# Attention scores: the keys' lower part laid twice over each other, so that both matmuls of a score use the same 128-row weights

## The chip, the core and the metric

One core of a Trainium2 chip runs the whole kernel. Its engines work through their own instruction lists side by side: TensorE (matmuls; its weight loads are listed apart), VectorE, ScalarE, GpSimd, and SyncE, which issues most of the DMA transfers. Times are device microseconds (us) of one execution; lower is better.

## The reference

One transformer block over 512 positions of width 1024, all in float32: a norm, a wide input projection, two branches (differential attention and a gated delta rule), a merge with gates, an output projection, an MLP and a gated embedding. The change is in the attention branch. It has 8 heads, each with two score maps of head size 64:

```python
s = jnp.einsum('bqhd,bkhd->bhqk', q_blk, k).astype(jnp.float32)
s = jnp.where(kpos[None, :] <= qpos[:, None], s, -jnp.inf)
w = jax.nn.softmax(s, axis=-1).reshape(b, DA_HEADS, 2, Q_BLOCK, t)
a = w[:, :, 0] - lam * w[:, :, 1]
return jnp.einsum('bhqk,bkhd->bqhd', a.astype(v.dtype), v)
```

The queries are worked through in 4 blocks of 128, and the scores are causal: block b needs the keys 0 to (b + 1) * 128.

## The kernel before, in words

Activations lie with channels on the 128 partitions and the 512 positions along the free dimension. Products that need float32 precision are made from float32r matmuls on split operands: a value is written as an upper part (`hi`) and a rest (`lo`). A dense tile (`dense_steps`) runs 8 times `hi` weights with `hi` and `lo` activations and then 8 times `lo` weights with `hi` activations, 24 matmuls of 512 columns. Weights come as `raw` by DMA from SyncE's queue (L106). In the long middle stage ScalarE casts the upper part (`whi`, L115) and writes its negative into `wlo` (L116), and a DMA from GpSimd's queue adds `raw` to it (L117).

The middle stage (up to about 790 us) mixes three kinds of work on TensorE in an order that the program writes out by its own estimate of matmul times (`run`, `step`, `fill`): the tiles of the input projection as filler, the attention of each head (`attn`), and the pieces of the delta rule (`gdn_a`, `gdn_i`, `gdn_u`, `gdn_s`, `gdn_n`). That order is fixed for TensorE; the other engines' lists and the addresses of the tiles are set by a scheduler and by memory pools.

A head h has 64 channels for score map s = 0 (partitions 0 to 63, `top`) and 64 for s = 1 (64 to 127, `bot`). `aq_tile` writes for each s a full tile `q[s]`: on the 64 partitions of s stands the upper part of q, on the other 64 its lower part. `ak_tile` writes for each s a full tile `kh[s]` (`k` in the rows): the upper part of k on its own 64 partitions (ScalarE, L679), and a copy of it on the other 64 (GpSimd, L681). So one 128-row matmul of `q[s]` with `kh[s]` gives q_hi k_hi + q_lo k_hi. The lower part of k stands in one tile `kl` (VectorE, L680), each s on its own 64 partitions, and a second matmul of only these 64 rows adds q_hi k_lo.

`attn` goes over b = 0 to 3 and, in it, over s: the two matmuls into a bank `psat` (at least 256 columns; the weights are 128 queries), a mask (L712), the row maximum (L713), and the exponential on ScalarE (L715). Then the two maps are combined into `aw`, transposed (`psaT`), copied to `aT` and multiplied with the values (`psao`). Between these steps the filler and the delta rule run. Right before b = 0 of a head, its `ak` tile has just been projected; the first score matmul waits for L679 to L681.

After the last head the remaining delta rule, 16 gate tiles (`gth`, stored in `g_d`) and the first loads of the next stage come together: `of`, the last head's output, is stored in `oa_d`; `ot` tiles are loaded from `oa_d` and split into `brh` (ScalarE, L98) and `brl` (VectorE, L99); the delta rule's `gdn_u` needs `Ye` and `Yx` (L533, L535) for its matmuls `psU`.

Of the kernel before, what the change touches and what calls it, by code (L numbers as in the profile page):

```python
# [8 lines left out]
F32 = mybir.dt.float32  # L9
F32R = mybir.dt.float32r  # L10
# [7 lines left out]
T = 512  # L18
# [19 lines left out]
def hybrid_block(ctx, tc, xT, pT, w1, wba, wa, wb, wo, wup, wdn, wple, wpg, vecs, rows, consts, out):  # L38
    nc = tc.nc
    V, S, PE, G = nc.vector, nc.scalar, nc.tensor, nc.gpsimd  # L40
    mult, add, sub, mx = ALU.mult, ALU.add, ALU.subtract, ALU.max
# [28 lines left out]
    def bc(ap, shape, axis):  # L70
        return ap.unsqueeze(axis).broadcast_to(shape)
# [3 lines left out]
    def mm(ps, lhsT, rhs, start=True, stop=True, **k):  # L75
        n = 1
        for i in rhs.shape[1:]:
            n *= i
        spent[0] += max(n / 2200.0, 0.025) if rhs.dtype == F32R else n / (1170.0 if k else 585.0)
        PE.matmul(ps, lhsT=lhsT, rhs=rhs, start=start, stop=stop, **k)  # L80

    def transpose(ps, src):
        mm(ps, src, ident, is_transpose=True)

    def rsqrt(pool, r, x, n):

        h = pool.tile([128, n], F32, name="nw_h")
        t = pool.tile([128, n], F32, name="nw_t")
        V.tensor_scalar(r.bitcast(I32), x.bitcast(I32), -0.5, 1597463007.0, op0=mult, op1=add)
        V.tensor_scalar(h, x, -0.5, None, op0=mult)  # L90
        for _ in range(3):
            V.tensor_tensor(t, r, r, op=mult)
            V.tensor_tensor(t, t, h, op=mult)  # L93
            V.scalar_tensor_tensor(r, in0=t, scalar=1.5, in1=r, op0=add, op1=mult)
# [61 lines left out]
    def newdense(src, a, kt=KD, lo=None, raw=None):  # L156
        w = load_w(src, kt, lo, raw)
        ps = pd.tile([128, T], F32, name="ps")
        dense(ps, w, a, kt)
        return ps  # L160
# [9 lines left out]
    with pool_("pro", bufs=2) as pool:  # L170
# [9 lines left out]
        for k in range(KD):  # L180
            q = ss if k == 0 else pool.tile([128, T], F32, name="sq")
# [12 lines left out]
        for d in range(KD):  # L194
            ps = newdense(wple[d], p2, 2, G, raw=raws[d] if d < 2 else None)
# [108 lines left out]
    apool = apool_.__enter__()  # L304
# [357 lines left out]
    at_ = {h: {} for h in range(8)}  # L662
# [11 lines left out]
    def ak_tile(h):  # L674
        def then(ps):
            kh = at_[h]["kh"] = [apool.tile([128, T], F32R, name=f"k{s}") for s in range(2)]
            kl = at_[h]["kl"] = apool.tile([128, T], F32R, name="kl")
            for s, hi, lo in ((0, top, bot), (1, bot, top)):
                S.copy(kh[s][hi], ps[hi])  # L679
                V.tensor_tensor(kl[hi], ps[hi], kh[s][hi].bitcast(F32), op=sub)  # L680
                G.tensor_copy(kh[s][lo], kh[s][hi])  # L681
        return ("ak", h), w1[8 + h], then, ("k_read", h - 1)

    def av_tile(h):
# [5 lines left out]
    def attn(h):  # L690
        d = at_.pop(h)
        q, kh, kl, vT = (d[n] for n in ("q", "kh", "kl", "vT"))
        psv = pt.tile([128, NC, 128], F32, name="psav", tag="t")
        for c in range(NC):
            transpose(psv[:, c], vT[:, c * 128:(c + 1) * 128])
        done.add(("av_read", h))
        vt = apool.tile([128, NC, 128], F32, name="vt", tag="vt")
        S.copy(vt, psv)
        oo = apool.tile([128, NC, 128], F32, name="oo")
        sso = apool.tile([128, NC], F32, name="asso")  # L700
        l2 = apool.tile([128, NC], F32, name="l2")
        yield 1.5
        for b in range(NC):
            n = (b + 1) * 128
            st = apool.tile([128, 4], F32, name="st", bufs=3)
            ws = []
            for s in range(2):
                pss = pt.tile([128, T], F32, name="psat", tag="t")
                m, hi, bs = max(n, 256), slice(64 * s, 64 * s + 64), slice(b * 128, n)
                mm(pss[:, :m], q[s][:, bs], kh[s][:, :m], stop=False)  # L710
                mm(pss[:, :m], q[s][hi, bs], kl[hi, :m], start=False)
                V.tensor_tensor(pss[:, b * 128:n], pss[:, b * 128:n], mqk, op=add)  # L712
                V.tensor_reduce(st[:, s:s + 1], pss[:, :n], axis=AX.X, op=mx, negate=True)  # L713
                w = apool.tile([128, T], F32, name="aw", bufs=3)
                S.activation(w[:, :n], pss[:, :n], AF.Exp, bias=st[:, s:s + 1], accum_out=st[:, 2 + s:3 + s])  # L715
                ws.append(w)
            if b == NC - 1:
                done.add(("k_read", h))

            rr = apool.tile([128, 1], F32, name="rr", bufs=3)  # L720
            V.reciprocal(rr, st[:, 3:4])
            V.scalar_tensor_tensor(rr, in0=rr, scalar=st[:, 2:3], in1=nlam, op0=mult, op1=mult)
            V.tensor_scalar(l2[:, b:b + 1], st[:, 2:3], st[:, 2:3], EPS, op0=mult, op1=mult)
            V.scalar_tensor_tensor(ws[0][:, :n], in0=ws[1][:, :n], scalar=rr, in1=ws[0][:, :n], op0=mult, op1=add)
            yield 6.0 + 0.5 * b
            psa = pt.tile([128, NC, 128], F32, name="psaT", tag="t")
            for kb in range(b + 1):
                transpose(psa[:, kb], ws[0][:, kb * 128:(kb + 1) * 128])
            aT = apool.tile([128, NC, 128], F32, name="aT", bufs=2)
            S.copy(aT[:, :b + 1], psa[:, :b + 1])  # L730
            yield 1.5
            pso = pt.tile([128, 128], F32, name="psao", tag="t")
            for kb in range(b + 1):
                mm(pso, aT[:, kb], vt[:, kb], start=kb == 0, stop=kb == b)
            V.tensor_copy(oo[:, b], pso)
            junk = apool.tile([128, 128], F32, name="ajunk")
            S.activation(junk, oo[:, b], AF.Square, accum_out=sso[:, b:b + 1])
            if b < NC - 1:
                yield 1.5
        V.scalar_tensor_tensor(sso, in0=sso, scalar=1.0 / 128.0, in1=l2, op0=mult, op1=add)  # L740
        rt = apool.tile([128, NC], F32, name="art")
        rsqrt(apool, rt, sso, NC)
        V.tensor_tensor(oo, oo, bc(rt, [128, NC, 128], 2), op=mult)
        yield 7.0
        psoT = pt.tile([128, T], F32, name="psaoT", tag="t")
        for c in range(NC):
            transpose(psoT[:, c * 128:(c + 1) * 128], oo[:, c])
        of = apool.tile([128, T], F32, name="of", tag="vt")
        S.activation(of, psoT, AF.Identity, scale=gsub)
        nc.sync.dma_start(oa_d[h], of)  # L750
# [8 lines left out]
    def units():  # L759
        for h in range(-1, 8):  # L760
            if h < 7:
                yield key_tile(h + 1)
                yield query_tile(h + 1)
                for i in range(2):
                    yield value_tile(h + 1, i)
                yield aq_tile(h + 1)
                yield av_tile(h + 1)
                yield ak_tile(h + 1)
            if h >= 0:
                yield gate_tile(h, 0)  # L770
                yield gate_tile(h, 1)
        for n in range(16):
            yield branch_gate(n)
# [3 lines left out]
    for h in range(8):  # L777
        chains.append([0.0, (("Z", h, 1), ("S", h)), gdn_n, h, ("B", h)])
        chains.append([0.0, (("U", h), ("B", h - 1)), gdn_s, h, ("S", h)])
        chains.append([0.0, (("I", h), ("U", h - 1)), gdn_u, h, ("U", h)])  # L780
        chains.append([0.0, (("ak", h), ("T", h - 1)), attn, h, ("T", h)])
        chains.append([0.0, (("V", h, 1), ("A", h - 1)), gdn_a, h, ("A", h)])
        chains.append([0.0, (("A", h), ("I", h - 1)), gdn_i, h, ("I", h)])
# [37 lines left out]
    h = hp.tile([128, KD, T], F32, name="h")  # L821

    with pool_("obp", bufs=1, side="right") as pool:
        b2 = branch(pool, ob_d, [*range(4, 8), *range(4)], pool, "ot", 2)
        m = []
# [4 lines left out]
        for d in range(KD):  # L830
            ps = pd.tile([128, T], F32, name="ps")
# [53 lines left out]
    for d in range(KD - NO):  # L885
        ps = newdense(wo[d], mg)
# [61 lines left out]
    for d in range(KD):  # L948
        ps = pd.tile([128, T], F32, name="ps")
# [16 lines left out]
    for d in range(KD - ND):  # L966
        ps = pd.tile([128, T], F32, name="ps")
# [38 lines left out]
    for sl in halves:  # L1006
        ss = new_ss()
        for d in range(KD):
            ps = pd.tile([128, T], F32, name="ps")
# [83 lines left out]
```

## Time and profile before

| | |
|---|---|
| time, median of 3 runs | 1423.91 us (1422.7 to 1426.05) |
| the profiled execution | 1418.5 us, of which its span 1416.7 us |
| mean granted TensorE clock | 0.985 of full speed |
| TensorE busy | 1343.1 us (95% of the span), 8402 matmuls |
| weight loads busy | 1101.9 us (78%) |
| VectorE busy | 801.6 us (57%) |
| ScalarE busy | 665.0 us (47%) |
| GpSimd busy | 213.6 us (15%) |

The profile lists what each engine did in one execution. Matmuls are pipelined: an entry's length reaches beyond the start of the next, so the distance from start to start is what a matmul takes of the stream. A weight load is an entry of its own (PEld) and can lie beside a running matmul. Idle time of an engine is put down to what ended it (the releaser).

### The profile page before, as it was taken

Reading aid. Unit: us, or ns where it says so; the run is one execution under the profiler, and the core shown is the slowest. Engines: PE = TensorE matmul, PEld = TensorE weight load, DVE = VectorE, ACT = ScalarE, POOL = GpSimd, SP = SyncE. Lnnn points to the kernel's source line nnn. Section 1 sums busy time; section 2 is a strip of 40 time slices with the busy share of each in tenths; the row PEclk is TensorE's granted clock in tenths of the full one; section 3 lists DMA queues with packets and bytes.
Section 4 is the critical chain, followed back from the end, with each engine's and each line's share of the span. In section 5 each row is a group of like instructions: output and inputs, shape, how many; then the busy total and the mean of one; then the engine's idle time right before and its main releaser. Section 6 shows DMA issues by size and latency. Waiting matters only on the chain.

```text
span 1416.7 us, 22558 instructions
## 1 busy us (share of the span) xinstructions
PE 1343.1 (95%) x8402; PEld 1101.9 (78%) x8402; DVE 801.6 (57%) x2132; ACT 665.0 (47%) x1354; POOL 213.6 (15%) x232
## 2 busy tenths in 40 slices
PE   6989999999999998999989999999999999999985
PEld 4767877777778776787768778898888888888985
DVE  6566695858768594876422443358443224434574
ACT  5656575666657574665545322254232223223241
POOL 3221111111211121120001000001421002200341
PEclk9999999999999999999989999999999999999997
DMA  7876555575655665574877753351122322323321
GB/s 258 186 185 140 140 138 145 142 172 135 163 137 132 146 138 144 130 162 118 228 181 186 247 184 120 118 194 53 52 98 90 102 92 90 98 96 104 111 83 60
DMA packets 94430, 194.65 MB, mean 137 GB/s; under 512 B 34000, under 2 KB 40528, under 8 KB 94320
## 3 DMA queue, kind: packets, MB, share of 16 engines
q1 hardware_dynamic: 81648, 147.07, 33.0%
q0 software_dynamic: 12672, 46.14, 17.6%
q8 instruction: 66, 1.08, 0.3%
q14 instruction: 44, 0.36, 0.1%
HBM read 130.19 MB, written 16.84 MB: 104 GB/s over the span
## 4 chain that ended last, share of the span: by engine, by line
PE 50%; DVE 5%; DMA 4%; ACT 1%; issue 1%; POOL 0%; SPq 0%; ACTq 0%; POOLq 0%; DVEq 0%
PE ps L80 45%; DMA ot<-ob_d 1%; DMA g_d<-gth 1%; DMA wlo<-raw 1%; DVE h L873 1%; DVE ht L872 1%; PE psat L80 1%; PE psS L80 0%; PE psO L80 0%; PE psV L80 0%; DVE ss L859 0%; PE psr L153 0%; PE psao L80 0%; PE pss L145 0%; DVE nw_t L93 0%
## 5 line engine op out<-in xcount | busy, mean ns | idle before, releaser
L80 PE MATMUL ps<-u_hi,whi 128*128 128x512 f32 (+1 forms) x952 | 384.3, 405 | 0.3 <-DVE mr L932 0.3
L80 PE MATMUL ps<-u_lo,whi 128*128 128x512 f32 (+1 forms) x952 | 371.5, 391 | 0.0
L80 PE MATMUL ps<-u_hi,wlo 128*128 128x512 f32 (+1 forms) x952 | 250.1, 396 | 4.3 <-DMA wlo<-raw 4.3
L80 PEld LDWEIGHTS ps<-u_hi,whi 128*128 128x128 f32 x952 | 180.9, 190 | 38.3 <-issue 2.1
L80 PEld LDWEIGHTS ps<-u_lo,whi 128*128 128x128 f32 x952 | 180.9, 190 | 33.3
L80 PEld LDWEIGHTS ps<-u_hi,wlo 128*128 128x128 f32 x952 | 173.0, 190 | 40.2 <-DMA wlo<-raw 5.5
L98 ACT CAST whi<-raw 128x1024 fp32r<-128x1024 f32 (+1 forms) x93 | 92.2, 993 | 228.3 <-PE ps L80 223.1
L99 DVE TENSOR_TENSOR wlo<-raw,whi 128x1024 fp32r<-128x1024 f32 x83 | 101.3, 1220 | 108.8 <-PE ps L80 88.2
L117 POOL DMA_DIRECT2D wlo<-raw x88 | 76.1, 864 | 491.5 <-ACT wlo L116 294.9
L115 ACT CAST whi<-raw 128x1024 fp32r<-128x1024 f32 x88 | 92.1, 1047 | 57.4 <-PE ps L80 56.0
L116 ACT ACTIVATE wlo<-whi 128x1024 fp32r<-128x1024 f32 x88 | 92.8, 1055 | 0.2
L80 PE MATMUL ps<-hid_hi,whi 128*128 128x512 f32 x224 | 88.5, 395 | 0.0
L80 PE MATMUL ps<-hid_lo,whi 128*128 128x512 f32 x224 | 88.4, 394 | 0.0
L80 PE MATMUL ps<-brh,whi 128*128 128x512 f32 x208 | 82.1, 396 | 0.5 <-ACT whi L98 0.5
L80 PE MATMUL ps<-brl,whi 128*128 128x512 f32 x208 | 82.1, 395 | 0.0
L369 DVE SCALAR_TENSOR_TENSOR acc<-ps,cw,acc 128x511 f32<-128x511 f32 (+2 forms) x96 | 71.3, 742 | 6.8 <-ACT acc L366 6.3
L934 POOL TENSOR_TENSOR mr<-mr 128x512 f32<-128x512 f32 (+1 forms) x37 | 39.3, 1063 | 216.6 <-ACT hid_hi L933 215.9
L932 DVE SCALAR_TENSOR_TENSOR mr<-ps,r 128x512 f32<-128x512 f32 (+1 forms) x37 | 22.9, 619 | 72.8 <-PE ps L80 69.3
L80 PE MATMUL ps<-hid_hi,wlo 128*128 128x512 f32 x224 | 56.9, 395 | 0.0
L80 PE MATMUL ps<-brh,wlo 128*128 128x512 f32 x208 | 52.6, 395 | 0.0
L80 PEld LDWEIGHTS ps<-hid_lo,whi 128*128 128x128 f32 x224 | 42.1, 188 | 10.3
L80 PEld LDWEIGHTS ps<-hid_hi,wlo 128*128 128x128 f32 x224 | 42.0, 188 | 10.3
(332 smaller groups left out, 2410.0 us busy)
## 6 DMA issues: line engine op xcount, KB each, us to landing
raw<-w SPq DMA_DIRECT2D x88, 512.0 KB, 3.5
wlo<-raw POOLq DMA_DIRECT2D x88, 512.0 KB, 4.8
raw<-wup SPq DMA_DIRECT2D x32, 512.0 KB, 3.3
raw<-wdn SPq DMA_DIRECT2D x32, 512.0 KB, 3.6
raw<-wb SPq DMA_DIRECT2D x16, 512.0 KB, 3.9
gB<-gcr_d SPq DMA_DIRECT2D x16, 256.0 KB, 4.2
bB<-ber_d SPq DMA_DIRECT2D x16, 256.0 KB, 4.9
ob_d<-zs SPq DMA_DIRECT2D x16, 256.0 KB, 3.6
```

The costliest lines, as they stand in the source:

```text
L80: PE.matmul(ps, lhsT=lhsT, rhs=rhs, start=start, stop=stop, **k)
L98: S.copy(hi, src)
L99: (eng or V).tensor_tensor(lo, src, hi.bitcast(F32), op=sub)
L115: S.copy(whi, raw)
L116: S.activation(wlo, whi.bitcast(F32), AF.Copy, scale=-1.0)
L117: nc.gpsimd.dma_start(wlo, raw, accum_op=add)
L369: V.scalar_tensor_tensor(acc[:, s:], in0=ps[:, :T - s], scalar=cw[:, j, w:w + 1], in1=acc[:, s:], op0=mult, op1=add)
L872: V.scalar_tensor_tensor(t, in0=psr, scalar=vec[:, g + d:g + d + 1], in1=y[:, d, sl], op0=mult, op1=mult)
L873: adds[d % len(adds)].tensor_tensor(h[:, d, sl], r, t, op=add)
L932: V.scalar_tensor_tensor(r[:, :n], in0=ps[:, :n], scalar=0.0, in1=r2[:, sl], op0=mx, op1=mult)
L934: G.tensor_tensor(r[:, :n], r[:, :n], r[:, :n], op=mult)
```

## The change

`kl` becomes two full tiles, `kl[0]` and `kl[1]`. Each holds the lower part of its score map's keys twice: on the 64 partitions where VectorE writes it, and, copied by GpSimd, on the other 64. The second matmul of a score then uses all 128 rows of `q[s]`, the same weights as the first. Beside q_hi k_lo it now adds q_lo k_lo, which the kernel before left out.

```diff
     def ak_tile(h):
         def then(ps):
             kh = at_[h]["kh"] = [apool.tile([128, T], F32R, name=f"k{s}") for s in range(2)]
-            kl = at_[h]["kl"] = apool.tile([128, T], F32R, name="kl")
+            kl = at_[h]["kl"] = [apool.tile([128, T], F32R, name=f"kl{s}") for s in range(2)]
             for s, hi, lo in ((0, top, bot), (1, bot, top)):
                 S.copy(kh[s][hi], ps[hi])
-                V.tensor_tensor(kl[hi], ps[hi], kh[s][hi].bitcast(F32), op=sub)
+                V.tensor_tensor(kl[s][hi], ps[hi], kh[s][hi].bitcast(F32), op=sub)
                 G.tensor_copy(kh[s][lo], kh[s][hi])
+                G.tensor_copy(kl[s][lo], kl[s][hi])
         return ("ak", h), w1[8 + h], then, ("k_read", h - 1)
...
-                m, hi, bs = max(n, 256), slice(64 * s, 64 * s + 64), slice(b * 128, n)
+                m, bs = max(n, 256), slice(b * 128, n)
                 mm(pss[:, :m], q[s][:, bs], kh[s][:, :m], stop=False)
-                mm(pss[:, :m], q[s][hi, bs], kl[hi, :m], start=False)
+                mm(pss[:, :m], q[s][:, bs], kl[s][:, :m], start=False)
```

TensorE's list has the same instructions in the same order before and after; only the height of 64 matmuls and their weight loads differs. The attention pool is larger by one tile of 128 x 512. The other lists change in a few places. On GpSimd, the first head's keys (`k`, `kl`), between two DMAs that finish weight tiles (`wlo`):

```order
 L117 DMA wlo_792<-raw_789 128x1024
 L681 COPY k_864<-k_864 64x512
-L117 DMA wlo_876<-raw_873 128x1024
+L682 COPY kl_866<-kl_866 64x512
+L117 DMA wlo_879<-raw_876 128x1024
 L681 COPY k_865<-k_865 64x512
+L682 COPY kl_867<-kl_867 64x512
 L429 TENSOR_TENSOR bB<-bB,dt 128x512
```

The weight DMA now stands behind the first `kl` copy, and the second `kl` copy behind the second `k` copy; the other seven heads read the same.

On ScalarE, behind the last head's output `of`, where the casts of `ot` (`brh`) meet the delta rule's `Yx` and `U`, first as it stood before:

```order
L749 ACTIVATE of<-psaoT,gsub 128x512
L98 CAST brh_8199<-ot 128x1024
L98 CAST brh_8201<-ot 128x1024
L115 CAST whi_8266<-raw_8264 128x1024
L755 ACTIVATE gth<-ps 128x512
L116 ACTIVATE wlo_8267<-whi_8266 128x1024
L115 CAST whi_8338<-raw_8336 128x1024
L98 CAST brh_8203<-ot 128x1024
L533 ACTIVATE Yx<-psY_8288,C 32x8x16
L98 CAST brh_8205<-ot 128x1024
L755 ACTIVATE gth<-ps 128x512
L533 ACTIVATE Yx<-psY_8288,C 32x8x16
```

and as it stands now:

```order
L750 ACTIVATE of<-psaoT,gsub 128x512
L115 CAST whi_8290<-raw_8288 128x1024
L756 ACTIVATE gth<-ps 128x512
L116 ACTIVATE wlo_8291<-whi_8290 128x1024
L98 CAST brh_8223<-ot 128x1024
L98 CAST brh_8225<-ot 128x1024
L115 CAST whi_8362<-raw_8360 128x1024
L533 ACTIVATE Yx<-psY_8312,C 32x8x16 x2
L756 ACTIVATE gth<-ps 128x512
L116 ACTIVATE wlo_8363<-whi_8362 128x1024
L542 COPY U_349<-psU_8370 16x8x16
L98 CAST brh_8227<-ot 128x1024
```

The first two casts moved from before a weight tile to behind it, and the third and fourth from before and between the two `Yx` to behind both. On SyncE's queue the first two loads of `ot` moved from ahead of the store of `of` to right behind it; on VectorE the third and fourth `brl` moved behind the `Ye` and the `U` copies.

## Rows read from the trace of the kernel before

**Rows 1.** Stretches: us, then busy (xcount) of each engine, TensorE's clock, DMA.

```profile
225.00:305.00 80.00, 77.19 (x599) 61.37 (x598) 57.72 (x193) 49.84 (x119) 12.61 (x15) 1.00 0.59 142
690.00:760.00 70.00, 63.48 (x501) 51.67 (x500) 19.44 (x48) 34.45 (x57) 7.74 (x9) 0.93 0.75 199
```

**Rows 2.** Waits of TensorE, 60 to 700 us: total us, times, longest.

```profile
PE psN L80 <- DVE vs L613: 3.9, 4, 1.7
...
PE ps L80 <- DMA wlo<-raw: 3.4, 2, 2.0
PE psat L80 <- POOL k L681: 3.4, 5, 1.6
...
PE psq L80 <- ACT kt L415: 0.3, 1, 0.3
```

**Rows 3.** Instructions on tile kl: ns min/median/max, first and last start, shapes.

```profile
L80 PEld LDWEIGHTS psat<-kl,q x64: 182/183/183, 86.9 to 674.8; 64*128 64x128 f32 x64
...
L680 DVE TENSOR_TENSOR kl<-ps,k x16: 682/689/695, 84.8 to 631.9; 64x512 fp32r<-64x512 f32 x16
```

**Rows 4.** Timeline of TensorE, two score blocks: start us, length us, instruction.

```profile
102.24 0.28 PE L80 MATMUL psat<-k,q 128*128 128x256 f32 x1
102.45 0.38 PE L80 MATMUL psat<-kl,q 64*128 64x256 f32 x1
102.77 0.38 PE L80 MATMUL psat<-k,q 128*128 128x256 f32 x1
...
103.39 0.50 PE L80 MATMUL ps<-u_hi,whi 128*128 128x512 f32 x1
103.73 0.40 PE L80 MATMUL ps<-u_lo,whi 128*128 128x512 f32 x1
103.96 0.39 PE L80 MATMUL ps<-u_hi,whi 128*128 128x512 f32 x1
...
346.22 0.40 PE L80 MATMUL psat<-k,q 128*128 128x512 f32 x1
...
347.83 0.50 PE L80 MATMUL ps<-u_hi,whi 128*128 128x512 f32 x1
```

**Rows 5.** Timeline of TensorE and its weight loads, 256 columns, delta rule.

```profile
669.56 0.28 PE L80 MATMUL psS<-Sh,kql 128*128 128x256 f32 x1
669.56 0.19 PEld L80 LDWEIGHTS psS<-Sl,kqh 128*128 128x128 f32 x1
669.67 0.28 PE L80 MATMUL psS<-Sl,kqh 128*128 128x256 f32 x1
...
669.79 0.28 PE L80 MATMUL psS<-Sh,kqh 128*128 128x256 f32 x1
```

**Rows 6.** Timeline of all engines where a head's first score block starts.

```profile
383.01 0.60 POOL L681 CAST k<-k 64x512 fp32r<-64x512 f32 x1 [5.42 <-ACT k L679]
...
383.18 0.68 DVE L680 TENSOR_TENSOR kl<-ps,k 64x512 fp32r<-64x512 f32 x1
...
384.26 0.85 POOL L117 DMA_DIRECT2D wlo<-raw  x1 [0.64 <-ACT U L542]
...
385.16 0.61 POOL L681 CAST k<-k 64x512 fp32r<-64x512 f32 x1
...
386.44 0.50 PE L80 MATMUL ps<-u_hi,whi 128*128 128x512 f32 x1
```

**Rows 7.** Timelines of SyncE, ScalarE, VectorE and TensorE behind the last head.

```profile
697.40 1.24 SPq L750 DMA_DIRECT2D oa_d<-of  x1
...
702.39 0.59 SPq L805 DMA_DIRECT2D ot<-oa_d  x1
...
709.28 1.04 ACT L98 CAST brh<-ot 128x1024 fp32r<-128x1024 f32 x1 [3.79 <-DMA ot<-oa_d]
710.35 1.23 DVE L99 TENSOR_TENSOR brl<-ot,brh 128x1024 fp32r<-128x1024 f32 x1 [5.46 <-ACT brh L98]
...
714.12 0.21 PE L80 MATMUL psU<-U,Yx 128*16 128x16 f32 x1 [1.86 <-ACT Yx L533]
```

## The prediction

> **What bounds the kernel now.** I read the busy time by stretch first [rows 1]. In a stretch that holds one attention head, 225 to 305 us, TensorE is busy 77.19 of 80 us, VectorE 57.72, ScalarE 49.84 and GpSimd 12.61: TensorE sets the pace, the others have room. The same view shows one weaker stretch, 690 to 760 us, just behind the last head: TensorE 63.48 of 70 us at a mean granted clock of 0.93.
>
> The waits of TensorE from 60 to 700 us come next [rows 2]. The largest item is 3.9 us; the list has 15, down to 0.3 us, and adds up to about 26 us. So in the attention stage a microsecond taken out of TensorE's own stream is mostly a microsecond of the span, if the stream really holds it. One item bears on the change: 3.4 us, five waits of the score matmuls for GpSimd's copies of `k`.
>
> Then the score matmuls themselves. The 64 matmuls with `kl` are 64 rows high, each with a weight load of its own of 183 ns [rows 3]; their neighbours are all 128 rows. The stream in order of time shows what this height does [rows 4]. A score block (both `s` of one `b`, four matmuls) of 256 columns starts at 102.24 and the next tile at 103.39: 1.15 us. Within it the starts are 0.21, 0.32 and then twice some 0.31 us apart (102.77 to 103.39). In a row of 128-row matmuls of the same 256 columns, each also with new weights, the starts are 0.11 to 0.12 us apart [rows 5]. There the load of the next weights (0.19 us) begins at the start of the matmul before and lies beside it; with `kl` the distance is the load plus the columns, 0.19 + 0.12 = 0.31: nothing lies beside. At 512 columns a block takes 346.22 to 347.83 = 1.61 us [rows 4], while dense matmuls of 512 columns start 0.23 us apart (103.73 to 103.96). So each change of height, into 64 rows and back out, costs one uncovered load, and it trails into the next tile: 103.39 to 103.73 is 0.34 instead of 0.23.
>
> **The change, part by part.**
>
> *Height.* All four matmuls become 128 rows high. A block of 256 columns then takes 4 x 0.12 = 0.48 instead of 1.15 us: 0.67 saved. At 512 columns 4 x 0.23 = 0.92 instead of 1.61: 0.69. I take 0.67 for each of the 32 blocks (8 heads, 4 `b`), and set the 8 blocks with b = 0 aside, because there GpSimd decides. 24 x 0.67 = 16.1 us. The trail behind a block, 0.34 - 0.23 = 0.11, goes where a 128-row float32r matmul follows; I count 15 such blocks, 15 x 0.1 = 1.5 us. That both matmuls now name the same weights is counted at nothing: dense pairs use the same weights twice already and still start 0.23 us apart. Bounds of this part: the full 32 x 0.67 + 32 x 0.11 = 25 us, and 0 if the load stays uncovered (a rival below).
>
> *Two more copies for each head.* The upper and lower half of `kl` are now each copied to the other half by GpSimd, 16 copies of the same kind as those of `k`, 0.6 us each. GpSimd's order becomes k, kl, weight DMA, k, kl. One head stands for the pattern [rows 6]. The first `k` copy begins at 383.01, VectorE's first `kl` ends at 383.86, so its copy runs to about 384.55; the weight DMA, at 384.26 before, begins about 384.6 and ends 385.45; the second `k` copy ends about 386.1, the second `kl` copy about 386.7. TensorE's last score matmul then starts at 386.8 and the next tile at 386.9, where it started at 386.44: this block loses 0.5 us. The same sum on the other seven heads gives +0.3, +0.25, +0.15, +0.15, 0, -0.1, and -0.5 for the head whose copies are long done. Together about +0.7 us. TensorE runs its list in order, so behind the waiting matmul stand the dense matmuls of the weight tile in work, and nothing else can step in. The weight DMA issued 0.35 us late is not counted: two waits for `wlo` in 620 us make 3.4 us in all [rows 2], so it normally lands early. VectorE's `kl` subtraction takes 682 to 695 ns in all 16 cases [rows 3], whether GpSimd copies beside it or not, so I price slower VectorE at 0, and at most at the copies' own length, 16 x 0.61 = 9.8 us.
>
> *What is late next.* A chain of VectorE and ScalarE work that spans a score block loses up to 0.67 us of cover, since its own length stays. Nothing if every chain had that much slack, all 16.9 us if none had. The list [rows 2] has about 20 waits of this kind against many more places where TensorE meets such a chain without waiting; I take one block in five, 3.4 us given back, near the end that the 96% busy TensorE speaks for.
>
> *The last head's tail.* The pool for attention is larger by one tile, and loads and splits of `ot` move there. Before, TensorE stood until 714.12 for `Yx` [rows 7]: ScalarE runs `Yx` behind a cast of `ot` that began at 709.28, on data whose load was issued at 702.39, 6.9 us earlier. After, the first two loads of `ot` are issued behind the store of `of` (issued at 697.40, 1.24 us), so at about 698.7, land 6.9 us later at 705.6, and their two casts of 1.04 us end at 707.7. VectorE's subtractions of 1.23 us each (row of 710.35) end at about 709.1, and the two `Ye` and `Yx` follow without another `ot` between them. TensorE goes on at about 710 instead of 714.1: about 4 us. The clock there (0.93 in the mean of 70 us, so part of the time at 1.2 instead of 2.4 GHz) may drop for as long as before. I take -3.5; the bounds are -7, if stall and clock loss both go, and +2, if the loads land later than I assume.
>
> *Order on VectorE elsewhere.* In the first head one `aw` moves behind an instruction that waits for a load; a `Uq` step or a transpose changes place with a neighbour in others. All feed waits that TensorE had there anyway, so they are priced at 0, with 2 us either way.
>
> **Sum.** -16.1 - 1.5 + 0.7 + 3.4 - 3.5 = -17.0 us. The profiled execution took 1418.5 us (span 1416.7, and 1.8 around it), so 1401.5 by its measure. The median of the runs is 5.4 us above it: 1423.91 - 17.0 = 1406.9, say 1407 us.
>
> **A rule that speaks against it.** Two 128-row matmuls with different weights follow each other at 0.12 us with the load inside that time [rows 5]. The Trainium skill says otherwise in one place: TensorE: Matmul & The Clock Gate, part 3 on packing small matmuls, has weight loads overlap matmuls in flight only when their row groups differ. By that rule a matmul on all 128 rows could never cover the next load, the distance would stay 0.31, and the first term would be 0 in place of 16.1. The rows disagree with it, so I go by the rows.
>
> **The rivals.**
>
> *Most of it is given back.* TensorE's time goes but chains become the bound: VectorE is at 57.72 of 80 us per head and has instructions waiting on each other. If three blocks in five hand their 0.67 back, 10.1 instead of 3.4 us, and the tail brings nothing, the change is -6.8: 1417 us. For it: the waits of TensorE are nearly all for VectorE, ScalarE and DMA. Against it: they total only 4% of the stage.
>
> *No cover, slower.* The uncovered load may come from the score tiles themselves (their weights `q`, their target banks) and not from the height. Then the first term is 0, and in seven of the eight b = 0 blocks the last matmul comes 0.61 us later because its `kl` copy stands behind the second `k` copy: +4.3 us with the tail as it was, 1428 us. It decides from the point where less than some 0.2 us of a block is saved. For it: the `k` matmul between two `kl` also starts 0.3 us after its neighbour. Against it: that is the first of 128 rows after one of 64, and the 128-row matmuls of `psS` run at 0.12 [rows 5].
>
> *Larger than thought.* All 32 trails and blocks count, no chain is late, and the tail frees its whole stall: -25 - 0 - 7 with the copies at +5 is about -27, 1397 us.
>
> **How the numbers follow.** My forecast, with its own range 1400 to 1413, gets 0.73; the give-back 0.15; the larger gain 0.07; no cover 0.05. The range for 8 in 10 is 1399 to 1416 us: it reaches into the give-back and leaves out the far ends. What a measurement of this kernel can tell from no change is about 0.2%, 2.8 us. Faster by more than that: forecast, larger gain and nearly all of the give-back, 0.93. Within: 0.03, from the rest of the give-back. Slower: 0.04, from no cover.
>
> **What would show it.** Right: no 64-row matmul on the score tiles; within a block from b = 1 on, starts 0.12 us (256 columns) and 0.23 us (512) apart; in b = 0 blocks the wait for GpSimd moved to the last matmul and longer by 0.3 to 0.6 us; a head some 2 us shorter; TensorE's wait for `Yx` in the tail ending earlier. Wrong: distances of 0.31 us between 128-row score matmuls; TensorE's waits for VectorE and ScalarE grown by more than 7 us over the stage; or a new wait of several microseconds in the tail.

## The result and the profile after

The changed kernel takes 1409.51 us (median of 4 runs, 1404.96 to 1412.98); the kernel before, on the same chip, 1423.47 us (1422.7 to 1426.05). The ratio is 0.9897, interval 0.9866 to 0.9928: 14.0 us faster. Two more comparisons of the same pair gave 0.989 (0.9854 to 0.9926; 15.8 us) and 0.9881 (0.9855 to 0.9908; 17.9 us). Predicted were 1407 us and -17.0, with a range of 1399 to 1416. The profiled execution of after took 1404.96 us (span 1403.2), 13.5 less than that of before.

The page's line of busy times, after (engine, busy us, share of the span, instructions):

```profile
PE 1326.9 (95%) x8402; PEld 1101.2 (78%) x8402; DVE 803.1 (57%) x2132; ACT 664.0 (47%) x1354; POOL 223.0 (16%) x248
```

There are as many matmuls as before; TensorE is busy with them for 16.2 us less, and GpSimd is busy for 9.4 us more, with the copies. The score tiles by name, after: line, engine, operation, count, then min/median/max ns, first and last start, shapes:

```profile
L80 PE MATMUL psat<-kl,q x64: 277/337/582, 84.1 to 664.5; 128*128 128x256 f32 x32, 128*128 128x384 f32 x16, 128*128 128x512 f32 x16
```

No score matmul is 64 rows high any more. A block of 256 columns in TensorE's list of after (start us, length, line, operation, shape, columns), where [rows 4] had 1.15 us:

```profile
165.97 0.28 PE L80 MATMUL psat<-k,q 128*128 128x256 f32 x1
166.09 0.28 PE L80 MATMUL psat<-kl,q 128*128 128x256 f32 x1
166.21 0.28 PE L80 MATMUL psat<-k,q 128*128 128x256 f32 x1
166.33 0.28 PE L80 MATMUL psat<-kl,q 128*128 128x256 f32 x1
166.45 0.28 PE L80 MATMUL psS<-Sh,kqh 128*128 128x256 f32 x1
```

And one of 512 columns, where it was 1.61 us:

```profile
343.57 0.40 PE L80 MATMUL psat<-k,q 128*128 128x512 f32 x1
343.81 0.40 PE L80 MATMUL psat<-kl,q 128*128 128x512 f32 x1
344.04 0.40 PE L80 MATMUL psat<-k,q 128*128 128x512 f32 x1
344.27 0.39 PE L80 MATMUL psat<-kl,q 128*128 128x512 f32 x1
344.51 0.39 PE L80 MATMUL ps<-u_hi,whi 128*128 128x512 f32 x1
344.74 0.40 PE L80 MATMUL ps<-u_lo,whi 128*128 128x512 f32 x1
```

The blocks take 0.48 us (165.97 to 166.45) and 0.94 us (343.57 to 344.51). The tile behind the second goes on at 0.23 us: there is no trail. Over all 32 blocks, from the first score matmul to the next other one and waits inside included, before takes 47.5 us and after 34.7. Of this the 8 blocks with b = 0 take 13.7 us before and 14.8 after, the other 24 take 33.7 and 19.9. The matmuls at their own pace (0.12, 0.175 and 0.232 us for 256, 384 and 512 columns) would be 20.7.

The head of [rows 6], after, on GpSimd, TensorE and the DMA it issues (in brackets the idle time before and what ended it):

```profile
379.59 0.60 POOL L681 CAST k<-k 64x512 fp32r<-64x512 f32 x1 [5.41 <-ACT k L679]
380.51 0.61 POOL L682 CAST kl<-kl 64x512 fp32r<-64x512 f32 x1 [0.32 <-DVE kl L680]
381.09 0.85 POOL L117 DMA_DIRECT2D wlo<-raw  x1
381.99 0.61 POOL L681 CAST k<-k 64x512 fp32r<-64x512 f32 x1
382.54 0.62 POOL L682 CAST kl<-kl 64x512 fp32r<-64x512 f32 x1
...
382.65 0.39 PE L80 MATMUL psat<-k,q 128*128 128x256 f32 x1 [0.87 <-POOL k L681]
383.22 0.39 PE L80 MATMUL psat<-kl,q 128*128 128x256 f32 x1 [0.17 <-POOL kl L682]
383.44 0.39 PE L80 MATMUL ps<-u_hi,whi 128*128 128x512 f32 x1
```

The order is the predicted one: k, kl, weight DMA, k, kl. The last score matmul waits for the last copy.

What TensorE waits for from 60 to 690 us, after (who waits, for whom: us in total, times, longest), against [rows 2]:

```profile
PE psN L80 <- DVE vs L613: 6.5, 4, 3.0
PE psat L80 <- POOL k L681: 4.9, 5, 1.8
PE psaoT L80 <- DVE eq L478: 4.1, 1, 4.1
...
PE psat L80 <- DVE oo L736: 1.9, 1, 1.9
...
PE psat L80 <- POOL kl L682: 1.1, 6, 0.2
```

The whole list grows from 26.1 to 33.4 us: the waits of `psat` from 4.1 to 8.8, the other waits for VectorE and ScalarE from 18.6 to 23.2.

The tail, after ([rows 7]), from the lists of SyncE's queue, ScalarE and TensorE:

```profile
684.98 0.32 SPq L751 DMA_DIRECT2D oa_d<-of  x1
685.46 1.10 SPq L806 DMA_DIRECT2D ot<-oa_d  x2
...
693.14 1.05 ACT L98 CAST brh<-ot 128x1024 fp32r<-128x1024 f32 x1 [1.91 <-DMA ot<-oa_d]
694.76 1.06 ACT L98 CAST brh<-ot 128x1024 fp32r<-128x1024 f32 x1 [0.57 <-DMA ot<-oa_d]
...
697.44 0.21 PE L80 MATMUL psU<-U,Ye 128*16 128x16 f32 x2 [1.06 <-DVE Ye L535]
698.61 0.19 PE L80 MATMUL psU<-U,Yx 128*16 128x16 f32 x1 [0.18 <-ACT Yx L533]
```

TensorE stands there for some 1.6 us in all, before for 6.5. From the end of the last score matmul to the last matmul into `psY`, also of the delta rule, it is 43.9 us, before 49.8. The clock of the 70 us there is 0.98, against 0.93 in [rows 1].

### The profile page after: what moved, and what is told of

Its sections match the earlier page's. It is cut to its first block, busy times and chain, and to the rows that moved or that the text cites. A ratio compares the mean times of both kernels' runs of the same rounds, so it can differ in the third digit from the quotient of the medians.

```text
span 1403.2 us, 22583 instructions
## 1 busy us (share of the span) xinstructions
PE 1326.9 (95%) x8402; PEld 1101.2 (78%) x8402; DVE 803.1 (57%) x2132; ACT 664.0 (47%) x1354; POOL 223.0 (16%) x248
## 4 chain that ended last, share of the span: by engine, by line
PE 44%; DVE 4%; DMA 4%; issue 1%; ACT 1%; SPq 0%; POOL 0%; ACTq 0%; POOLq 0%; DVEq 0%
PE ps L80 41%; DMA ot<-ob_d 1%; DMA g_d<-gth 1%; DVE h L874 1%; DMA wlo<-raw 1%; DVE ht L873 1%; DMA ot<-oa_d 1%; DVE ss L860 0%; PE psr L153 0%; DVE brl L99 0%; PE pss L145 0%; ACT brh L98 0%; DVE nw_t L93 0%; DVE nb_r L94 0%; PE psO L80 0%
```

## The experiments

The changed kernel differs from before in three things at once: the height of the second matmul, the copies of `kl`, and a pool with one more tile, which reorders the lists. The first batch (before at 1425.93 us) takes them one at a time.

### The pool alone: kl in two tiles, still 64 rows

```diff
-kl = apool.tile([128, T], F32R, name="kl")
+kl = [apool.tile([128, T], F32R, name=f"kl{s}") for s in range(2)]
...
-mm(pss[:, :m], q[s][hi, bs], kl[hi, :m], start=False)
+mm(pss[:, :m], q[s][hi, bs], kl[s][hi, :m], start=False)
```

> The kernel before with kl in two tiles of 128 x 512 instead of one, each used only on its own 64 partitions: matmuls 64 rows high as before, no copies of kl. Only the attention pool grows, and with it the lists of the other engines change as they do in the changed kernel, the tail behind the last head included. Theory (the height is the gain, the tail a small extra): score blocks still 1.15 us at 256 columns, TensorE's stall for Yx in the tail shorter, 2 to 6 us faster than before, about 0.997. Rival (the order of the lists made most of the gain): 10 us or more faster, 0.993 or below. Rival (the order brings nothing): 1.000.

Measured: 1419.3 us, ratio 0.9962 (0.9938 to 0.9985). The medians differ by -6.6 us; the ratio would make it -5.4. Its blocks take 49.6 us as a sum, much as before. The tail is short here too: from the last score matmul to `psY` 43.7 us. TensorE's list of this kernel, `psU`:

```profile
710.20 0.21 PE L80 MATMUL psU<-U,Ye 128*16 128x16 f32 x2 [0.68 <-DVE Ye L535]
```

So some 5 to 7 us of the gain have nothing to do with the weights. They come with the order of loads and casts that the larger pool brings; the tail alone is 6.1 us shorter in this profile.

### The height alone: zeros in the other half, no copies

Against the changed kernel:

```diff
+kls = [apool.tile([128, T], F32R, name=f"kl{s}") for s in range(2)]
+G.memset(kls[s][lo].bitcast(F32), 0.0)          # once
...
-G.tensor_copy(kl[s][lo], kl[s][hi])
```

> The changed kernel without its copies of kl: the two kl tiles are allocated once, the half that VectorE doesn't write is filled with zeros once at the start, and the 128-row matmul adds zero there (so q_lo k_lo is left out as it was before). Theory (height): blocks of 0.48 us at 256 columns as in the changed kernel, and in the first block of each head no wait for kl: 0.1 to 0.5 us less there for each of seven heads, 2 to 3 us faster than the changed kernel, about 0.988 of before. Rival (the copies cost much more, by holding up the weight DMAs behind them): 6 us or more faster than the changed kernel, 0.985 or below. Rival (the copies cost nothing, since the block waits for the copy of k anyway): the same as the changed kernel, 0.990.

Measured: 1405.78 us, 0.9865 (0.9842 to 0.9889), -20.2 us. Against `two64`, which has as large a pool and was run in the same batch, the height is worth 13.5 us. The blocks fall from 49.6 to 29.9 us. (The tiles with zeros are also allocated once and not for each head; no run takes this apart.)

### The copies alone: changed kernel with 64-row matmuls

```diff
-mm(pss[:, :m], q[s][:, bs], kl[s][:, :m], start=False)
+mm(pss[:, :m], q[s][hi, bs], kl[s][hi, :m], start=False)
```

> The changed kernel with its copies of kl, but the second matmul reads only the 64 rows of its own half, as before (nothing reads the copied halves). Theory (height): blocks of 1.15 us again; no matmul waits for the copies, so they cost only GpSimd's time: as fast as the kernel with two tiles and no copies within 2 us, about 0.997 of before. Rival (copies hold up weight DMAs): 3 us or more slower than that kernel, 1.000 or above.

Measured: 1419.02 us, 0.9961 (0.9939 to 0.9983): the same as `two64`. 16 copies on GpSimd cost nothing that these medians can tell, as long as no matmul waits for them.

### Same weights, or same height?

The 64-row pairs are grouped by height, k, k, kl, kl; the same grouping with 128 rows (and zeros) takes away neighbours with equal weights.

```diff
+for s in range(2): mm(psc[s][:, :m], q[s][:, bs], kh[s][:, :m], stop=False)
+for s, hi in ((0, top), (1, bot)): mm(psc[s][:, :m], q[s][hi, bs], kl[s][hi, :m], start=False)   # group64
+for s, hi in ((0, top), (1, bot)): mm(psc[s][:, :m], q[s][:, bs], kl[s][:, :m], start=False)     # group128
```

> 64-row matmuls in two tiles without copies, but in each block both 128-row matmuls first, then both 64-row matmuls (rows 0 to 63, then rows 64 to 127). Theory (what costs is the change of height): only two changes in a block instead of four; starts at 256 columns about 0.12, 0.21, 0.12 and 0.31 us apart, a block of 0.76 us, 0.35 us less than before in 24 or more blocks, 8 to 10 us faster than the kernel with two tiles. Rival (a 64-row load is never covered): the third distance is 0.31 as well, a block of 0.95. Rival (the load of another group of rows runs beside the matmul): third distance 0.12 or below. The first exponential of a block starts later by one matmul, which may give 1 or 2 us back.

> The kernel with zeros in the other half of kl (128 rows, no copies of kl), but in each block both matmuls with k first, then both with kl: no two neighbours have the same weights any more. Theory (height): still 0.12 us from start to start at 256 columns and 0.23 at 512, blocks of 0.48 and 0.93 us. Rival (the same weights are what saves): a load of 0.19 us uncovered between the matmuls, 0.31 us apart, blocks near 1.1 us and 12 us or more slower than the kernel with zeros. The first mask and exponential of a block start one matmul later, so a time 0 to 3 us above the kernel with zeros, about 0.988 of before.

Measured: `group64` 1410.05 us, 0.9897 (0.9872 to 0.9922). `group128`, in the second batch (before 1424.25 us), 1405.7 us, 0.9873 (0.9842 to 0.9903), against 1405.78 for `zero` in the first batch and 1402.56 for the same kernel in the third (`zero2`, below). A block of `group128` in TensorE's list (x2: two matmuls drawn together):

```profile
167.37 0.40 PE L80 MATMUL psat<-k,q 128*128 128x256 f32 x2
167.61 0.40 PE L80 MATMUL psat<-kl,q 128*128 128x256 f32 x2
167.85 0.28 PE L80 MATMUL psS<-Sh,kqh 128*128 128x256 f32 x1
```

Four matmuls in 0.48 us, as in after, though no neighbour uses the weights of the one before: that both matmuls of a score name the same weights is worth nothing in the block. A block of `group64`, matmuls and weight loads (PEld):

```profile
238.37 0.40 PE L80 MATMUL psat<-k,q 128*128 128x256 f32 x2
...
238.69 0.19 PEld L80 LDWEIGHTS psat<-kl,q 64*128 64x128 f32 x2
238.69 0.38 PE L80 MATMUL psat<-kl,q 64*128 64x256 f32 x2
239.00 0.19 PEld L80 LDWEIGHTS ps<-U,Y 128*64 128x64 f32 x2
```

0.64 us where I expected 0.76. The two 64-row matmuls take 0.32 us together, a load of 0.19 and one matmul's 0.12: they lie side by side, one on the upper and one on the lower rows. This is the second rival of the expectation, a load that runs beside the matmul of another group of rows. The Trainium skill, TensorEngine Tiling (Array Packing), Key Properties, says that a change of tiling mode drains TensorE, and that different tiles can load and multiply in parallel. The rows agree with both. In these rows a block that changes height four times costs 0.67 us more than one of full height, and one that does so twice 0.16 more (0.64 against 0.48), with the 0.12 us already taken off that the two matmuls side by side save.

### What the copies cost the changed kernel

The changed kernel was run in three comparisons and the version with zeros in two; the third (before 1424.16 us) has both at once.

> The changed kernel once more, on the same chip as the three beside it. All theories: 0.990 of before, within 0.003.

> The changed kernel beside the kernel with zeros on one chip, to tell what its copies of kl cost. All theories: 0.990 of before, within 0.003.

> The kernel with zeros beside the changed kernel. Theory (the copies cost the waits for kl in seven first blocks, 0.4 us each, and the order on VectorE in the first head): 2 to 4 us faster than the changed kernel. Rival (nothing, as something else holds TensorE in those blocks): within 1 us of it.

Measured: the changed kernel 1408.41 (`again`) and 1406.27 us (`again2`); `zero2` 1402.56 us, 0.9836 (0.9811 to 0.9862), 3.7 us below `again2`. It is the fastest version here. The two intervals still overlap a little; over all executions the changed kernel has a mean of 1408.0 us (16) and the version with zeros 1403.4 (11). TensorE's `psat` waits sum to 8.7 us in `again2` and 5.2 in `zero2`, about the difference. But 1.9 us of it is one wait for `oo` in the first head; `two64`, which has no copies, waits 1.4 us there, so this part may be the order of the lists and not the copies. `zero2` leaves out q_lo k_lo, as the kernel before does.

### Attempts to buy cover

With `zero`, the largest wait is `psN` for `vs` (6.8 us), the next `psat` for the copies of `k` (4.3). Three edits of it go at them.

```diff
-G.tensor_copy(kh[s][lo], kh[s][hi])     # zero_act: k's copy by ScalarE from PSUM
+S.copy(kh[s][lo], ps[hi])
-yield 2.0                               # zero_act_y3: also psN planned 1 us later
+yield 3.0
-yield 1.5                               # zero_late: zero, first score matmul 1 us later
+yield 2.5
```

> The kernel with zeros, and the copies of k to the other half written by ScalarE straight from PSUM instead of by GpSimd behind it. Theory (in a head's first block TensorE waits for GpSimd's second copy, which stands behind a weight DMA): the 4.3 us of waits for GpSimd's k go, ScalarE's two casts more cost up to 1 us a head where something waits for ScalarE; 1 to 3 us faster than the kernel with zeros, about 0.985 of before. Rival (ScalarE's queue is as late, since the copy stands behind its other work): the waits move to ScalarE and the time is the same.

> The kernel before this one, and the delta rule's psN matmuls are planned one microsecond later behind their psV (3.0 instead of 2.0 in the program's own estimate), so that more dense matmuls stand between. Theory (part of the gain was given back because chains on VectorE lost cover when the score blocks became shorter, psN <- vs above all: 5.5 us before, 8.1 us after): the waits for psN fall below 3 us, 2 to 4 us faster than the kernel without this, about 0.983 of before. Rival (the state's chain is the bound and only shifts): the waits turn up at psS or psV and the time is the same within 2 us.

> The kernel with zeros, and the first score matmul of each head planned one microsecond later behind the transposes of the values (2.5 instead of 1.5 in the program's estimate). Theory (TensorE waits 4.3 us for GpSimd's second copy of k in five heads, and three or more dense matmuls of 0.23 us placed ahead fill that wait): the waits for k fall below 1.5 us, 2 to 4 us faster than the kernel with zeros. Rival (the later score chain runs into the head's next steps): the waits move to psaT, psN or psS and the time is the same within 2 us or worse.

Measured: `zero_act` 1408.52 us, 0.9896 (0.9861 to 0.9931), no better than `zero`; `zero_act_y3` 1423.34 us, 0.9997 (0.9975 to 1.0018); `zero_late` 1421.37 us, 0.9975 (0.996 to 0.999). None was faster than `zero`, so my theory fell in all three. TensorE's waits of `zero_act`:

```profile
PE psat L80 <- ACT k L684: 8.6, 7, 1.6
PE psN L80 <- DVE vs L613: 5.8, 3, 2.9
```

The wait for `k` went from GpSimd to ScalarE and doubled. Those of `zero_late`:

```profile
PE psaoT L80 <- DVE nw_t L92: 4.6, 1, 4.6
PE psS L80 <- ACT Sh L98: 4.3, 3, 2.2
PE psN L80 <- DVE vs L613: 4.0, 4, 1.6
```

`psat`'s wait for `k` has fallen to 0.4 us, as expected, but a different order of the whole stage has put other chains at the head of the list. From 60 to 800 us TensorE's waits rise from 38.4 (`zero`) to 45.8 us, and the granted clock, read in slices of 5 us from 85 to 800, loses 18.9 us of full speed in place of 11.9: together 14 of the 15.6 us between the two. The clock's part is not a matter of one execution: over all of them the mean granted clock is 0.978 in `zero_late` and 0.982 in `zero`, some 7 us of full speed. In `zero_act_y3` the waits of `psN` for `vs` fell below 3 us as well (2.0), but it has 9.1 us more waits in all than `zero_act`, at no more loss of clock, and is 14.8 us slower; the rest stays open.

## Why the prediction was right, step by step

**Height, -16.1, and trail, -1.5: the mechanism as predicted, the sum smaller.** Blocks of 0.48 and 0.94 us were forecast at 0.48 and 0.92. The rival "no cover, slower" is out: a load lies beside a 128-row matmul whether the weights are new (`group128`) or not. The 24 blocks from b = 1 on gave 13.8 us (33.7 to 19.9) in place of 16.1; the new wait for `oo` in the first head, 1.9 us, lies in one of them. The trails, from the start of the next matmul to the one behind it, gave 2.8 us in place of 1.5, since more blocks had one than the 15 counted. With the blocks of b = 0, that is 15.6 against 16.9 forecast for height, trail and copies together. Without copies (`two64` to `zero`) the blocks alone gave 19.7, of which the median kept 13.5.

**Two more copies, +0.7: near in the blocks that it was worked out for; against zeros they cost 3.7 us.** The term was the change of the blocks with b = 0 against before, and these grew by 1.1 us (13.7 to 14.8). The block that I worked out, +0.5, came out at +0.42 (2.06 us, 381.38 to 383.44, in place of 1.64). The `psat` waits for GpSimd are 4.9 + 1.1 us against 3.4. The 3.7 us are another difference: with zeros these blocks take 11.2 (`zero`) and 10.9 us (`zero2`), so the copies use up what the height would save there. VectorE's `kl` subtraction stayed at 682 to 695 ns (median 689), so the 9.8 us bound was never touched.

**What is late next, +3.4: right for the waits; a second cost, the clock, was left out, and is small in the median.** TensorE's other waits for VectorE and ScalarE grew by 4.6 us (18.6 to 23.2). The kernels with 64-row matmuls have 18.6, 18.9 and 19.8 us of them; the changed kernel and those with zeros 23.2, 20.2, 21.7, 24.7 and 23.8. The means are 19.1 and 22.7: +3.6. What I left out is the clock. It shows behind a chain of the delta rule in the second head, TensorE's list of after:

```profile
180.92 0.40 PE L80 MATMUL ps<-u_lo,whi 128*128 128x512 f32 x1
184.29 0.95 PE L80 MATMUL psN<-vs,kt 128*128 128x256 f32 x2 [2.97 <-DVE vs L613]
...
185.75 0.77 PE L80 MATMUL ps<-u_hi,whi 128*128 128x512 f32 x1
186.32 0.63 PE L80 MATMUL ps<-u_lo,whi 128*128 128x512 f32 x1
186.75 0.63 PE L80 MATMUL ps<-u_hi,whi 128*128 128x512 f32 x1
```

The same stretch by slices (from:to, length, then busy us of TensorE, weight loads, VectorE, ScalarE, GpSimd with counts; granted clock, DMA share, GB/s):

```profile
183.00:184.00 1.00, 0.00 (x0) 0.00 (x0) 1.00 (x3) 0.55 (x1) 0.00 (x0) 1.00 1.05 197
...
185.00:186.00 1.00, 1.00 (x6) 0.96 (x5) 0.70 (x3) 0.00 (x0) 0.00 (x0) 0.50 0.03 12
186.00:187.00 1.00, 1.00 (x4) 0.80 (x4) 0.87 (x4) 0.81 (x3) 0.00 (x0) 0.50 0.98 262
...
188.00:189.00 1.00, 1.00 (x6) 0.84 (x5) 0.86 (x5) 1.00 (x2) 0.00 (x0) 1.00 0.02 8
```

Behind the wait of 2.97 us the granted clock is 0.50 (1.2 in place of 2.4 GHz), until about 188 us, and dense matmuls start 0.43 us apart instead of 0.23. In before the longest wait at `psN` was 1.7 us, and the stretch with this piece kept its clock; TensorE was busy for 3.25 of its 5 us:

```profile
185.00:190.00 5.00, 3.25 (x16) 2.54 (x16) 4.72 (x17) 2.70 (x7) 0.00 (x0) 1.00 0.69 159
```

Such a dip costs 1.7 us of full speed. Which wait has one behind it is not settled: in before, one of 1.64 us that ended at 418.5 has, and one of 1.61 us that ended at 553.3 has not. Summed over slices of 5 us from 85 to 675, the clock lost 5.1 us in before (3 dips) and 8.6 in after (5); `two64` lost 1.7, `zero` 11.9. From the first to the last score block after saves 7.8 us (588.5 to 580.7). Of the 15.6 saved in blocks and trails, 7.8 were thus handed back in these two executions; longer waits outside the blocks (4.6) and clock (3.4) make 8.0 by these counts.

In the median the clock's share is smaller. The span and the mean granted clock of every execution are on record; the span times what the clock lacks to full speed is 23.8 us in the mean for `two64` and `copies64` (24 executions), 24.8 for the changed kernel (16) and 24.2 for zeros (11). So at the same short tail 128 rows lost about 1 us more, no more than the scatter of these means. Before lost 26.9 (57 executions of the experiments), with the low clock of its tail in it. So by these counts most of what was handed back are the waits.

**The tail, -3.5: -6.6 measured, with the order elsewhere in it.** The steps were right: `ot` loaded right behind the store of `of`, 7.7 us from load to cast (6.9 assumed), no third cast ahead of `Yx`. Most of the stall went (6.5 to 1.6 us), and part of the clock loss with it. The -6.6 is `two64` by medians (its ratio makes -5.4); it lies between the value taken and the bound of -7, and shows this part apart from the rest.

**Order on VectorE elsewhere, 0 with 2 either way: up to 2.3 us lost in the first head.** VectorE's list there, of before:

```profile
90.04 0.35 DVE L724 SCALAR_TENSOR_TENSOR aw<-aw,rr 128x128 f32<-128x128 f32 x1
```

and of after:

```profile
92.13 0.81 DVE L502 TENSOR_TENSOR tmpq<-L,Uq 128x15 f32<-128x15 f32 x1 [4.61 <-DMA L<-ld_d]
92.86 0.34 DVE L725 SCALAR_TENSOR_TENSOR aw<-aw,rr 128x128 f32<-128x128 f32 x1
```

`aw`, which ran ahead of the wait for `L`, now stands behind it; in `two64` and `zero`, which have no copies, it still runs ahead. From its first to its third score block this head took 28.8 us before and 31.1 after, but 29.0 and 29.7 in `again` and `again2`, the same kernel. This is a part of the waits above, not beside them.

**The sum.** By differences of medians: height net -13.5, copies +3.7, order and tail -6.6 make -16.4; the three comparisons gave -14.0, -15.8 and -17.9. In the terms of the forecast, height, trail, copies and what is late next were to bring -13.5 (-16.1 - 1.5 + 0.7 + 3.4) and brought -9.8 (-13.5 + 3.7), since more was handed back than the 3.4; the tail was to bring -3.5 and brought -6.6. In the main the mechanism of each was the predicted one. That the sum came out within 3 us is partly luck: two parts were off by 3.7 and 3.1 us to opposite sides. "Most of it is given back" (-6.8) and "larger than thought" (-27) are both away from what was measured, though without the larger pool the gain would have been nearer to the first.

## What to carry to other kernels

Between matmuls of one height the next weight load costs nothing here; a matmul of fewer rows between full ones costs an uncovered load on the way in and on the way out, so fill the missing rows, with zeros if nothing useful is at hand, and don't pay for copies that TensorE has to wait for. Once TensorE's own stream shrinks, price the chains beside it: the wait that grows, and the lower clock that can stand behind it. The clock came to about 1 us here, and to some 7 in `zero_late`, so take it from many executions and not from one profile. And look at what an edit does to pools and list order apart from its purpose: here that was a third of the gain or more.

## What was not expected of the hardware

Two 64-row matmuls on different halves of the rows ran side by side: load and both matmuls took 0.32 us at 256 columns in `group64`, against 0.31 us for each one in before. At 512 columns its whole block took 0.99 us (131.94 to 132.93), hardly more than 0.94 with full height. The Trainium skill, TensorE: Matmul & The Clock Gate, part 3, lets weight loads overlap matmuls in flight, in its list of what overlaps, only if their row groups differ; the paragraph ahead of that list also allows a load into a background weight buffer. Blocks of 0.48 us, in which loads of 0.19 us for all rows lie beside matmuls on all rows, don't agree with the list, so the measurement decides; which buffer a load goes to, no run here shows.
